# Inputs of a decoder layer laid out on the host: x by columns, parameters by columns, weights by loads

## The chip, the cores and the metric

One core of a Trainium2 chip runs the kernel. The metric is the device time in microseconds (us). Three runs of the kernel before are given by their median; one more run was profiled.

## The reference

One decoder layer on `x` (1 x 256 x 1024, float32). With one block of 256 keys, no past block can be chosen, so the block-sparse attention is causal attention over 16 heads of 64, with a relative-position bias on the logits. A gated feed-forward part with a causal width-3 depthwise convolution follows, and a last RMS norm.

```python
h = x
y = rms_norm(h, attn_norm)                    # x * rsqrt(mean(x^2) + eps) * g
q, k, v = split(y @ w_qkv)                    # 1024 -> 3 * 1024
s = q @ k.T * 64 ** -0.5 + bias(distance)     # causal
h = h + softmax(s) @ v @ w_o
y = rms_norm(h, ffn_norm)
u = conv3(y @ w_up) + conv_b                  # 1024 -> 2 * 2816, F = 2816
gate, val = split(u)
h = h + (silu(gate) * val) @ w_down           # 2816 -> 1024
out = rms_norm(h, final_norm)
```

## The kernel before, in words

Each product is made of three float32r products, high times high, low times high and high times low, so every weight is split into a high part (`whi`, on ACT, L175) and a low part (`wlo`, mostly on DVE, L194), and the activations too (`yt`, high on ACT at L298, low on DVE at L301). Weights come in loads of 1 MB into four `raw` buffers (`load`, L98), in a fixed order: four loads for v (each two blocks of 128 rows of the v part of `w_qkv`), then pairs for q and k (`qc`, `kc`, each 256 columns of all 1024 rows), then `w_o`, `w_up` and `w_down`. SP issues them; a load waits until its buffer has been split. The engines take their instructions in the order in which the program was recorded: nothing is reordered later.

The v product comes first. For each of the eight blocks of 128 features (k = 0 to 7), TensorE multiplies `yt` of that block with its weight rows into four accumulators `acc` (L349, L386): 12 products of 128x512 per block. `yt` needs x with features on partitions. x is loaded by rows (`xs`, L225), TensorE transposes it block by block against `ident` into a `bank` of PSUM (L289, L294), and ACT and DVE scale it by `g1` and split it from there. `g1` is `attn_norm` by columns: loaded as a row (L230), transposed (L259), scaled by ACT (L260). The other small vectors (`ffn_norm`, `conv_w`, `conv_b`) are loaded as `rows` (L246) and transposed in the middle of the v stage (`other_params`, L262).

The norm's factor is not needed for `yt`: it is put on q, k and v afterwards. `stat` gets the sums of squares of the two row halves of x from ACT (L428, L430), `rstds` (L276) turns them into `r1` with one DVE (L279) and one POOL instruction (L280), and just ahead of the products of the last block TensorE spreads `r1` over the partitions (`spread(r1, bank())`, L418, L286). After that, the first q and k products follow at once. Before the first product, TensorE runs some products of `ones` (`keep_warm`, L317).

At the end (L883 to L906) the last norm is put on four pieces of the output, and four DMAs store them: `by_final` (L853) multiplies a piece by `final_norm`, `weighted` (L841) does so for the rows of the second half, and `scale_of` (L847) gives the last factor `rf` through DVE (L849) and POOL (L850).

Of the kernel before, what the change touches and what calls it, by code (L numbers as in the profile page):

```python
# [14 lines left out]
P = 128  # L15
# [19 lines left out]
WARM = 6  # L35
MORE_WARM = 2
# [12 lines left out]
def tile_block(ctx: ExitStack, tc, x, attn_norm, w_qkv, w_o, rel_bias, ffn_norm, w_up, conv_w,  # L49
               conv_b, w_down, final_norm, out):  # L50
# [27 lines left out]
    wq, wo, wu, wd = w_qkv[0], w_o[0], w_up[0], w_down[0]  # L78
    ROWED = ("v", "o", "d", "s")
    first_tail = NG - TAIL  # L80
    blocks_of = wd[2 * first_tail * P:, :].rearrange("(i k p) (h c) -> k h p i c", k=2, p=P, h=2)
# [6 lines left out]
    def block(name):  # L88
        return blocks_of[int(name[0]) - 1, int(name[1]) - 1]

    def by_block(t):
        return t.rearrange("p (i c) -> p i c", i=TAIL)

    def add_block(t, name):
        more = block(name) if isinstance(name, str) else by_block(raws["s", name])
        nc.gpsimd.dma_start(by_block(t), more, accum_op=ALU.add)  # L96

    def load(key):  # L98
        kind, i = key
        if kind == "s":  # L100
            t = fp.tile([P, 2048], F32, name=f"sum{i}") if i in EARLY_SUMS else wraw.tile([P, 2048], F32, name="raw")
            nc.sync.dma_start(by_block(t), block(STAGES[i][0]))
            for name in STAGES[i][1:]:
                add_block(t, name)
            raws[key] = t
            return
        t = wraw.tile([P, 2048], F32, name="raw")
        if kind in ROWED:
            src = {"v": wq[:, 2 * D:], "o": wo, "d": wd}[kind][2 * i * P:2 * (i + 1) * P, :]
            dst, src = t.rearrange("p (k c) -> p k c", k=2), src.rearrange("(k p) c -> p k c", p=P)  # L110
        else:
            w, base = {"qc": (wq, 0), "kc": (wq, D), "gc": (wu, 0), "uc": (wu, F)}[kind]
            src = w[:, base + 256 * i:base + 256 * (i + 1)].rearrange("(k p) c -> p k c", p=P)
            dst = t.rearrange("p (k c) -> p k c", k=KD)
        if key == ("v", 0):
            load_x(0, 2 * P)
            for r in range(2):
                nc.sync.dma_start(dst[:, r, :], src[:, r, :])
            load_x(2 * P, 2 * P)
        elif key == ("v", 1):  # L120
            nc.sync.dma_start(dst[:, 0, :], src[:, 0, :])
            load_x(4 * P, 4 * P)
            nc.sync.dma_start(dst[:, 1, :], src[:, 1, :])
        else:
            nc.sync.dma_start(dst, src)
        raws[key] = t
# [50 lines left out]
    def split_lo():  # L177
        n, u = divmod(state["lo"], 2)
        if state["lo"] == state["hi"]:
            return  # L180
        state["lo"] += 1
        g = groups[n]
        src = parts(g)[u]
        lo[g, u] = wsp.tile([P, 1024], F32R, name="wlo", bufs=UNITS)
        if g in ADDED_LOW:
            nc.scalar.activation(lo[g, u], hi[g, u].bitcast(F32), AF.Copy, scale=-1.0)  # L186
            if g[0] == "d":
                k = 2 * g[1] + u
                nc.gpsimd.dma_start(lo[g, u], wd[k * P:(k + 1) * P, :], accum_op=ALU.add)
            else:  # L190
                nc.gpsimd.dma_start(lo[g, u].rearrange("p (i c) -> p i c", i=2),  # L191
                                    block(STAGES[g[1]][0])[:, 2 * u:2 * u + 2, :], accum_op=ALU.add)
# [32 lines left out]
    def load_x(b, n):  # L225
        c = slice(b, b + n)
        nc.sync.dma_start(xs[:, :, c], x[0, :, c].rearrange("(t p) c -> p t c", p=P))

    row1 = const.tile([KD, P], F32, name="row1")
    nc.scalar.dma_start(row1, attn_norm[0].rearrange("(k p) -> k p", p=P))  # L230
# [5 lines left out]
    rows = const.tile([P, 2, P], F32, name="rows")  # L236
# [3 lines left out]
    nc.vector.memset(rows[64:, :, :], 0.0)  # L240
    ROWS = {"w0": (0, 0), "w1": (0, 2 * NF), "g2": (0, 4 * NF), "w2": (1, 0), "b": (1, 2 * NF)}
    for name, src in (("g2", ffn_norm[0]), ("b", conv_b[0]), ("w0", conv_w[0, 0]), ("w1", conv_w[0, 1]),
                      ("w2", conv_w[0, 2])):
        i, r = ROWS[name]
        n = src.shape[0] // P
        nc.sync.dma_start(rows[r:r + n, i, :], src.rearrange("(k p) -> k p", p=P))  # L246

# [4 lines left out]
    params = const.tile([P, 2, P], F32, name="params")  # L252
    g2 = params[:, 0, 4 * NF:4 * NF + KD]

    g1 = const.tile([P, KD], F32, name="g1")

    def first_params():
        ps = bank()
        nc.tensor.transpose(ps[:, :KD], row1, ident[:KD, :KD])  # L259
        nc.scalar.activation(g1, ps[:, :KD], AF.Copy, scale=math.sqrt(D))  # L260

    def other_params():  # L262
        ps = spare()[:, :2 * P].rearrange("p (a b) -> p a b", a=2)
        for i in range(2):
            nc.tensor.transpose(ps[:, i, :], rows[:, i, :], ident)
        nc.scalar.activation(params, ps, AF.Copy)
        nc.scalar.activation(g2, g2, AF.Copy, scale=math.sqrt(D))
# [8 lines left out]
    def rstds():  # L276

        r = small.tile([P, NT], F32, name="rstd")
        nc.vector.scalar_tensor_tensor(r, stat[:, 0, :], D * EPS, stat[:, 1, :], op0=ALU.add, op1=ALU.add)  # L279
        nc.gpsimd.tensor_tensor(r, r, minus_half.to_broadcast([P, NT]), op=ALU.pow)  # L280
        return r
# [7 lines left out]
    def flipped_rows(k, ps=None):  # L289

        ps = (bank() if ps is None else ps).rearrange("p (a b) -> p a b", a=2)
        for a in range(2):
            for t in range(NT):
                nc.tensor.transpose(ps[:, a, t * P:(t + 1) * P], xt[t][:, (k + a) * P:(k + a + 1) * P], ident)  # L294
        return ps

    def columns_hi(ps, k, g, a):
        nc.scalar.activation(yt[:, 0, k + a, :], ps[:, a, :], AF.Copy, scale=g[:, k + a:k + a + 1])  # L298

    def columns_lo(ps, k, g, a):  # L300
        nc.vector.scalar_tensor_tensor(yt[:, 1, k + a, :], ps[:, a, :], g[:, k + a:k + a + 1],  # L301
                                       yt[:, 0, k + a, :].bitcast(F32), op0=ALU.mult, op1=ALU.subtract)

    def transposed(k, g, ps=None):

        ps = flipped_rows(k, ps)
        for part in (columns_hi, columns_lo):
            for a in range(2):
                part(ps, k, g, a)
# [12 lines left out]
    first_params()  # L322


    line = const.tile([H, LGT], F32, name="line")
    nc.gpsimd.memset(line[:, S:], NEG)
# [14 lines left out]
    att = ctx.enter_context(ExitStack())  # L341
    ap = att.enter_context(tc.tile_pool(name="ap", bufs=1))
# [52 lines left out]
    columns_lo(ps, 0, g1, 0)  # L395
    columns_hi(ps, 0, g1, 1)
    half_lo(0, 0)
    columns_lo(ps, 0, g1, 1)
    half_lo(0, 1)
    half_hi(1, 0, nc.scalar.copy)  # L400
    half_hi(1, 1, nc.vector.tensor_copy)
    for half in range(2):
        half_lo(1, half)
    for half in range(2):
        for n in range(2):
            first_products(half, hi, n)
# [3 lines left out]
    for i in range(4):  # L410
        if i < 3:
            transposed(2 * i + 2, g1)
        if i == 2:
            other_params()
# [12 lines left out]
        if i == 1:  # L427
            nc.scalar.activation(junk[0], xt[0], AF.Square, accum_out=stat[:, 0, 0:1])  # L428
        if i == 2:
            nc.scalar.activation(junk[1], xt[1], AF.Square, accum_out=stat[:, 0, 1:2])  # L430
            r1 = rstds()
# [51 lines left out]

    def weights():
        return ap.tile([P, 768], F32, name="weights", bufs=6)
# [167 lines left out]
    def squares(t, half):  # L653
        c = slice(half * 512, (half + 1) * 512)
        nc.scalar.activation(junk[t][:, c], xt[t][:, c], AF.Square, accum_out=stat[:, half, t:t + 1])
# [23 lines left out]
    def taps(col):  # L679
        return tuple(params[:, i, r + col:r + col + 1] for i, r in (ROWS[n] for n in ("w0", "w1", "w2", "b")))  # L680
# [197 lines left out]
    for o, c in lefts:  # L878
# [17 lines left out]
    by_final(nc.vector, c_last)  # L896
    nc.sync.dma_start(rows_of(0, left), xg[0][:, left])
    square(1, c_last, 1, last)
    r = scale_of(1, 1)
    weighted(1, c_last, last)  # L900
    c = slice(0, 576)
# [7 lines left out]
_INS = ["x", "attn_norm", "w_qkv", "w_o", "rel_bias", "ffn_norm", "w_up", "conv_w", "conv_b", "w_down",  # L909
        "final_norm"]  # L910
_OUTS = [((1, S, D), "float32")]

# [21 lines left out]
```

## Time and profile before

| what | value |
|---|---|
| median of three runs | 295.5 us (295.25 to 296.05) |
| profiled execution's own time | 295.74 us |
| its span in the profile | 293.9 us, granted TensorE clock 0.994 |
| TensorE (PE) | 285.8 us busy, 97% |
| VectorE (DVE) | 238.9 us busy, 81% |
| ScalarE (ACT) | 185.0 us busy, 63% |
| GpSimd (POOL) | 47.1 us busy, 16% |
| DMA | 71.51 MB in 48886 packets, mean 243 GB/s |
| first product of the v stage / first q product | 6.21 us / 30.28 us |
| last instructions issued | 290.28 us |

The profile's times count from the start of the span. The time of a run is 1.84 us more than the span in the profiled execution. Lines L... are those of the kernel before; the changed kernel has other numbers for the same lines, which are named where they are used.

### The profile page before, as it was taken

Reading aid. Unit: us, or ns where it says so; the run is one execution under the profiler, and the core shown is the slowest. Engines: PE = TensorE matmul, PEld = TensorE weight load, DVE = VectorE, ACT = ScalarE, POOL = GpSimd, SP = SyncE. Lnnn points to the kernel's source line nnn. Section 1 sums busy time; section 2 is a strip of 40 time slices with the busy share of each in tenths; the row PEclk is TensorE's granted clock in tenths of the full one; section 3 lists DMA queues with packets and bytes.
Section 4 is the critical chain, followed back from the end, with each engine's and each line's share of the span. In section 5 each row is a group of like instructions: output and inputs, shape, how many; then the busy total and the mean of one; then the engine's idle time right before and its main releaser. Section 6 shows DMA issues by size and latency. Waiting matters only on the chain.

```text
span 293.9 us, 5514 instructions
## 1 busy us (share of the span) xinstructions
PE 285.8 (97%) x2092; PEld 264.3 (90%) x2092; DVE 238.9 (81%) x449; ACT 185.0 (63%) x328; POOL 47.1 (16%) x72
## 2 busy tenths in 40 slices
PE   7999999999999999999999999999999999999991
PEld 6888999989978789998999899988999989998881
DVE  3866978679698586899899919999796997898884
ACT  4585746556564676477566807675449679955842
POOL 3905008329100002001000100000012002302001
PEclk9999999999999999999999999999999999999997
DMA  7999597898896862378995999849959986976303
GB/s 222 413 386 361 175 327 218 265 373 189 285 349 164 305 246 77 113 234 283 273 354 191 326 270 264 287 137 310 386 99 328 257 326 224 228 128 116 98 0 143
DMA packets 48886, 71.51 MB, mean 243 GB/s; under 512 B 1933, under 2 KB 37085, under 8 KB 48733
## 3 DMA queue, kind: packets, MB, share of 16 engines
q1 hardware_dynamic: 43564, 59.97, 59.6%
q0 software_dynamic: 3696, 9.99, 16.5%
q10 hardware_dynamic: 1600, 1.22, 1.6%
q8 instruction: 16, 0.26, 0.3%
q14 instruction: 10, 0.07, 0.1%
HBM read 66.29 MB, written 3.83 MB: 239 GB/s over the span
## 4 chain that ended last, share of the span: by engine, by line
PE 82%; issue 11%; ACT 2%; DMA 1%; POOL 1%; DVE 0%; POOLq 0%; SPq 0%; ACTq 0%
PE acc L74 37%; PE bank L74 37%; PE spare L74 7%; DMA raw<-in_w_qkv_dram 1%; ACT wlo L186 1%; PE acc L294 1%; PE bank L294 0%; POOL wlo L191 0%; POOL raw L833 0%; ACT whi L175 0%; ACT cv L729 0%; POOL raw L854 0%; DVE u L725 0%; ACT raw L891 0%; ACT raw L905 0%
## 5 line engine op out<-in xcount | busy, mean ns | idle before, releaser
L74 PE MATMUL bank<-yt,whi 128*128 128x256 f32 x704 | 120.3, 276 | 0.0
L74 PEld LDWEIGHTS bank<-yt,whi 128*128 128x128 f32 x704 | 105.9, 188 | 0.0
L175 ACT ACTIVATE whi<-raw 128x1024 fp32r<-128x1024 f32 x94 | 94.1, 1048 | 16.4 <-DMA raw<-in_w_qkv_dram 6.6
L194 DVE TENSOR_TENSOR wlo<-raw,whi 128x1024 fp32r<-128x1024 f32 x82 | 99.2, 1235 | 2.3 <-ACT whi L175 1.4
L74 PE MATMUL bank<-yt,wlo 128*128 128x256 f32 x352 | 97.2, 276 | 0.0
L74 PEld LDWEIGHTS bank<-yt,wlo 128*128 128x128 f32 x352 | 66.1, 188 | 0.0
L729 ACT ACTIVATE cv<-u,params 128x256 f32<-128x256 f32 x44 | 24.1, 594 | 50.7 <-DVE u L725 50.7
L74 PE MATMUL acc<-whi,at 128*128 128x512 f32 (+1 forms) x128 | 33.9, 383 | 0.0
L74 PEld LDWEIGHTS acc<-whi,at 128*128 128x128 f32 x128 | 23.5, 188 | 4.4
L74 PE MATMUL acc<-yt,whi 128*128 128x256 f32 x160 | 27.3, 276 | 0.0
L725 DVE TENSOR_TENSOR u<-bank,rb 128x512 f32<-128x512 f32 x22 | 15.1, 688 | 13.1 <-PE bank L74 13.1
L74 PEld LDWEIGHTS acc<-yt,whi 128*128 128x128 f32 x160 | 24.1, 188 | 0.0
L746 DVE SCALAR_TENSOR_TENSOR cv<-u,params,cv 128x254 f32<-128x254 f32 x44 | 21.3, 483 | 1.6
L74 PE MATMUL acc<-yt,wlo 128*128 128x256 f32 x80 | 22.1, 276 | 0.0
L744 DVE SCALAR_TENSOR_TENSOR cv<-u,params,cv 128x255 f32<-128x255 f32 x44 | 21.0, 478 | 0.7 <-ACT cv L729 0.7
L74 PE MATMUL acc<-whi,ot 128*128 128x512 f32 x64 | 20.2, 396 | 0.0
L74 PE MATMUL acc<-wlo,at 128*128 128x512 f32 (+1 forms) x69 | 20.0, 367 | 0.0
L74 PE MATMUL acc<-whi,yt 128*128 128x512 f32 x64 | 17.6, 399 | 1.1 <-DVE whi L380 1.1
L508 ACT ACTIVATE weights<-weights,nz 128x128 f32<-128x128 f32 (+1 forms) x32 | 14.1, 443 | 5.6 <-DVE nz L504 5.6
L74 PE MATMUL spare<-yt,whi 128*128 128x256 f32 (+1 forms) x96 | 16.8, 279 | 0.0
L96 POOL DMA_DIRECT2D sum<-in_w_down_dram x3 | 3.9, 1309 | 77.5 <-DVE wlo L194 55.8
L74 PEld LDWEIGHTS acc<-wlo,at 128*128 128x128 f32 x69 | 13.0, 188 | 2.6
(164 smaller groups left out, 401.7 us busy)
## 6 DMA issues: line engine op xcount, KB each, us to landing
raw<-in_w_up_dram SPq DMA_DIRECT2D x22, 1024.0 KB, 7.6
raw<-in_w_qkv_dram SPq DMA_DIRECT2D x10, 1024.0 KB, 8.2
raw<-in_w_down_dram SPq DMA_DIRECT2D x10, 1024.0 KB, 5.7
raw<-in_w_o_dram SPq DMA_DIRECT2D x4, 1024.0 KB, 5.7
sum<-in_w_down_dram SPq DMA_DIRECT2D x3, 1024.0 KB, 8.6
sum<-in_w_down_dram POOLq DMA_DIRECT2D x3, 1024.0 KB, 10.0
wlo<-in_w_down_dram POOLq DMA_DIRECT2D x6, 512.0 KB, 9.4
weights<-turned SPq DMA_DIRECT2D x7, 384.0 KB, 4.4
```

The costliest lines, as they stand in the source:

```text
L74: nc.tensor.matmul(o, lhsT, rhs, start=start, stop=stop, skip_group_check=True)
L96: nc.gpsimd.dma_start(by_block(t), more, accum_op=ALU.add)
L175: nc.scalar.activation(like(hi[g, u], src), src, AF.Copy)
L186: nc.scalar.activation(lo[g, u], hi[g, u].bitcast(F32), AF.Copy, scale=-1.0)
L194: state["by"].tensor_tensor(like(lo[g, u], src), src, like(hi[g, u].bitcast(F32), src), op=ALU.subtract)
L294: nc.tensor.transpose(ps[:, a, t * P:(t + 1) * P], xt[t][:, (k + a) * P:(k + a + 1) * P], ident)
L508: nc.scalar.activation(sc[p][:, a, c], sc[p][:, a, c], AF.Exp, bias=nm[:, j], accum_out=z[:, j])
L725: nc.vector.tensor_tensor(u, ps, rb2.unsqueeze(1).to_broadcast([P, 2, S]), op=ALU.mult)
L729: nc.scalar.activation(c[:, a, :], u[:, a, :], AF.Identity, scale=w2, bias=b)
L744: nc.vector.scalar_tensor_tensor(c[:, a, 1:], u[:, a, :S - 1], w1, c[:, a, 1:], op0=ALU.mult, op1=ALU.add)
L746: nc.vector.scalar_tensor_tensor(c[:, a, 2:], u[:, a, :S - 2], w0, c[:, a, 2:], op0=ALU.mult, op1=ALU.add)
```

## The change

Before the launch, `kernel()` now arranges the inputs with numpy: `x_cols` is x with features on partitions (128 x 8 x 256), beside x itself; `cols` holds all small vectors by columns (128 x 192); and the weights are arrays in which every load is one contiguous run of 8 KB per partition. In the program:

- The transposes of x for the v stage, those of the parameters, `row1`, `rows` and their loads are gone. `yt` is made from `x_cols` in SBUF (`column(k)`, held in three buffers that the attention uses later). The transposes of the second norm stay.
- ACT's queue issues the load of `cols` (into `params`) and then that of block 0 of `x_cols`. SP's queue issues the other blocks among the loads for v, and x by rows (`xs`, 1 MB), which only the sums of squares and the residual read, after the last load for v.
- Both sums of squares stand after the third pair of blocks (before: one after the second pair, one after the third). The factor 1/D goes into the squares in place of sqrt(D) in the gains.
- `WARM` is 8, in place of 6 and 2 more.
- At the end, the last `by_final` stands behind the last `weighted`, in place of ahead of the second `square`.
- Empty tiles (`lead`, `rest`, `pad`) shift addresses.

```diff
-        if key == ("v", 0):
-            load_x(0, 2 * P)
-            for r in range(2):
-                nc.sync.dma_start(dst[:, r, :], src[:, r, :])
-            load_x(2 * P, 2 * P)
...
+        pieces = {("v", 0): (512, 512, (1, 2), 1024, (2, 3)), ("v", 1): (1024, (3, 6), 1024, (6, KD))}.get(key, (2048,))
+        at_column = 0
+        for piece in pieces:
+            if isinstance(piece, tuple):
+                load_columns(nc.sync, *piece)
+            else:
+                c = slice(at_column, at_column + piece)
+                nc.sync.dma_start(t[:, c], src[:, c])
+                at_column = c.stop
+        if key == ("v", 3):
+            nc.sync.dma_start(xs, x[0].rearrange("(t p) c -> p t c", p=P))
...
-    row1 = const.tile([KD, P], F32, name="row1")
-    nc.scalar.dma_start(row1, attn_norm[0].rearrange("(k p) -> k p", p=P))
+    params = const.tile([P, 2 * KD + 8 * NF], F32, name="params")
+    nc.scalar.dma_start(params, cols)
+    load_columns(nc.scalar, 0, 1)
     load_next()
...
-    ps = flipped_rows(0)
-    keep_warm(MORE_WARM)
+    columns_hi(column(0), 0, g1)
     half_hi(0, 0, nc.vector.tensor_copy)
-    columns_hi(ps, 0, g1, 0)
     half_hi(0, 1, nc.scalar.copy)
...
     for i in range(4):
-        if i < 3:
-            transposed(2 * i + 2, g1)
-        if i == 2:
-            other_params()
+        for k in (2 * i + 2, 2 * i + 3):
+            if k < KD:
+                columns_hi(column(k), k, g1)
+                columns_lo(column(k), k, g1)
...
-        if i == 1:
-            nc.scalar.activation(junk[0], xt[0], AF.Square, accum_out=stat[:, 0, 0:1])
         if i == 2:
-            nc.scalar.activation(junk[1], xt[1], AF.Square, accum_out=stat[:, 0, 1:2])
+            for t in range(NT):
+                nc.scalar.activation(junk[t], xt[t], AF.Square, scale=D ** -0.5, accum_out=stat[:, 0, t:t + 1])
             r1 = rstds()
...
     weighted(1, c, y)
-    by_final(nc.vector, c_last)
-    nc.sync.dma_start(rows_of(0, left), xg[0][:, left])
     square(1, c_last, 1, last)
     r = scale_of(1, 1)
     weighted(1, c_last, last)
+    by_final(nc.vector, c_last)
+    nc.sync.dma_start(rows_of(0, left), xg[0][:, left])
```

How this moves instructions is seen at three places. In the rows below, `DMAHW0` to `DMAHW7` are the semaphores that the loads raise in turn, and a wait on one is a wait for a landing. First, the start of ACT's queue, before:

```order
L230 DMA row1_90<-in_attn_norm_dram 8x128
L260 ACT_TABLE_LOAD
L260 ACTIVATE g1_119<-bank_133 128x8 [waits PE_49]
L298 ACTIVATE yt_121<-bank_189,g1_119 128x256 [waits PE_49,Activation_49]
L380 CAST whi_185<-raw_92 128x512 [waits DMAHW2_49]
```

and now (`DMAHW2` is block 0 of `x_cols`, `DMAHW0` the parameters):

```order
L230 DMA params_97<-in_cols_dram 128x192
L227 DMA weights_94<-in_x_cols_dram 128x256
L276 ACT_TABLE_LOAD [waits DMAHW2_49]
L276 ACTIVATE yt_123<-weights_94,params_97 128x256 [waits DMAHW0_49]
L357 CAST whi_185<-raw_100 128x512 [waits DMAHW3_49]
```

ACT's table load stood in front of every wait; now it stands behind the landing of block 0 of `x_cols`. Second, ACT's queue in the second half of the v stage, before (`raw_103` is the last load for v, `raw_220` the first for q, `raw_251` the first for k):

```order
L175 ACTIVATE whi_292<-raw_103 128x1024 [waits DMAHW1_49]
L428 ACTIVATE junk0_124,stat_123<-xs_89 128x1024 [waits DMAHW6_49,DMAHW4_49]
L298 ACTIVATE yt_121<-bank_299,g1_119 128x256 [waits PE_49]
L298 ACTIVATE yt_121<-bank_299,g1_119 128x256
L266 ACTIVATE params_118<-spare_308 128x256 [waits PE_49]
L267 ACTIVATE params_118<-params_118 128x8 [waits Activation_49]
L175 ACTIVATE whi_337<-raw_103 128x1024
L175 ACTIVATE whi_341<-raw_220 128x1024 [waits DMAHW7_49]
L430 ACTIVATE junk1_125,stat_123<-xs_89 128x1024
L175 ACTIVATE whi_379<-raw_251 128x1024 [waits DMAHW0_49]
```

and now (`raw_113` the last for v, `raw_213` the first for q, `raw_239` the first for k):

```order
L166 ACTIVATE whi_275<-raw_113 128x1024 [waits DMAHW4_49]
L276 ACTIVATE yt_123<-weights_96,params_97 128x256 [waits DMAHW2_49]
L276 ACTIVATE yt_123<-weights_96,params_97 128x256
L166 ACTIVATE whi_309<-raw_113 128x1024
L166 ACTIVATE whi_313<-raw_213 128x1024 [waits DMAHW6_49]
L404 ACTIVATE junk0_126,stat_125<-xs_89 128x1024 [waits DMAHW5_49]
L404 ACTIVATE junk1_127,stat_125<-xs_89 128x1024
L166 ACTIVATE whi_352<-raw_239 128x1024 [waits DMAHW7_49]
```

Both squares now stand behind the split of the first q load, which SP issues behind `xs`. Third, the last instructions of DVE, before:

```order
L842 TENSOR_TENSOR raw_3349<-acc_1742,raw_3348 128x256
L854 TENSOR_TENSOR raw_3349<-raw_3349,raw_3348 128x256
L849 SCALAR_TENSOR_TENSOR rf_3523<-ends1_3352 128x1 [waits DVE_49,Activation_49]
L842 TENSOR_TENSOR raw_3349<-bank_3465,raw_3348 128x256
L902 TENSOR_SCALAR raw_3349<-raw_3349,rf_3523 128x576 [waits DVE_49,Pool_49]
```

and now:

```order
L814 TENSOR_TENSOR raw_3322<-acc_1715,raw_3321 128x256
L821 SCALAR_TENSOR_TENSOR rf_3494<-ends1_3325 128x1 [waits DVE_49,Activation_49]
L814 TENSOR_TENSOR raw_3322<-bank_3438,raw_3321 128x256
L826 TENSOR_TENSOR raw_3322<-raw_3322,raw_3321 128x256
L874 TENSOR_SCALAR raw_3322<-raw_3322,rf_3494 128x576 [waits DVE_49,Pool_49]
```

The factor `rf` now comes one instruction of 256 columns earlier, and the store of the left half of the first rows (L897) one or two later.

More of the change, by code (lines that the diff above doesn't have):

```diff
@@ L48, in tile_block @@
 @with_exitstack
-def tile_block(ctx: ExitStack, tc, x, attn_norm, w_qkv, w_o, rel_bias, ffn_norm, w_up, conv_w,
-               conv_b, w_down, final_norm, out):
+def tile_block(ctx: ExitStack, tc, x, x_cols, cols, w_v, w_qk, w_o, rel_bias, w_up, w_down, w_tail,
+               final_norm, out):
     nc = tc.nc
@@ L223, in tile_block, with weights, column, load_columns @@
     xt = [xs[:, t, :] for t in range(NT)]
-    def load_x(b, n):
-        c = slice(b, b + n)
-        nc.sync.dma_start(xs[:, :, c], x[0, :, c].rearrange("(t p) c -> p t c", p=P))
-    row1 = const.tile([KD, P], F32, name="row1")
-    nc.scalar.dma_start(row1, attn_norm[0].rearrange("(k p) -> k p", p=P))
+    att = ctx.enter_context(ExitStack())
+    ap = att.enter_context(tc.tile_pool(name="ap", bufs=1))
+    ap.tile([P, 48], F32, name="lead")
+    def weights():
+        return ap.tile([P, 768], F32, name="weights", bufs=6)
+    columns = [weights() for _ in range(3)]
+    def column(k):
+        return columns[k // 3][:, k % 3 * S:(k % 3 + 1) * S]
+    def load_columns(queue, k0, k1):
+        t, c = divmod(k0, 3)
+        dst = columns[t][:, c * S:(c + k1 - k0) * S]
+        queue.dma_start(dst.rearrange("p (k s) -> p k s", k=k1 - k0), x_cols[:, k0:k1, :])
+    params = const.tile([P, 2 * KD + 8 * NF], F32, name="params")
+    nc.scalar.dma_start(params, cols)
+    load_columns(nc.scalar, 0, 1)
     load_next()
@@ L250, in tile_block @@
     nc.gpsimd.memset(minus_half, -0.5)
[L252 to L267, printed above, removed]
+    g1, g2 = params[:, :KD], params[:, KD:2 * KD]
+    TAPS = [2 * KD + 2 * NF * n for n in range(4)]
     act.tile([P, 48], F32, name="skew")
@@ L308, in transposed @@
             for a in range(2):
[L309 removed]
+                part(ps[:, a, :], k + a, g)
     junk = [act.tile([P, D], BF16, name=f"junk{t}") for t in range(NT)]
@@ L321, in tile_block @@
     keep_warm(WARM)
-    first_params()
     line = const.tile([H, LGT], F32, name="line")
+    const.tile([P, 72], F32, name="rest")
     nc.gpsimd.memset(line[:, S:], NEG)
@@ L654, in squares @@
         c = slice(half * 512, (half + 1) * 512)
-        nc.scalar.activation(junk[t][:, c], xt[t][:, c], AF.Square, accum_out=stat[:, half, t:t + 1])
+        nc.scalar.activation(junk[t][:, c], xt[t][:, c], AF.Square, scale=D ** -0.5,
+                             accum_out=stat[:, half, t:t + 1])
     for t in range(NT):
@@ L922 @@
     arrays, args = {}, []
-    for name in _INS:
-        a = _np.ascontiguousarray(inputs[name])
+    for name, a in _laid({k: _np.asarray(v) for k, v in inputs.items()}).items():
+        a = _np.ascontiguousarray(a)
         arrays[f"in_{name}_dram"] = a
```

111 lines of the change are left out of this document (52 added, 59 removed).

## The prediction

> **What bounds the kernel now.** I read the page's busy times first, then what TensorE (PE) waited for, then the chain of work that ended last. PE is busy for 97% of the span, and its list of waits has two rows, both before the first product of the v stage:
>
> ```profile
> span 293.9 us, 5514 instructions
> PE 285.8 (97%) x2092; PEld 264.3 (90%) x2092; DVE 238.9 (81%) x449; ACT 185.0 (63%) x328; POOL 47.1 (16%) x72
> PE acc L74 <- DVE whi L380: 1.1, 1, 1.1
> PE spare L74 <- DVE ones L239: 1.0, 1, 1.0
> ```
>
> So from the first product to the last, PE has work ready all the time. The time is the start, plus PE's own stream, plus the tail. The other engines and the DMAs matter only where a change makes PE wait for them. The pieces of the chain in the v stage (start, length, what) show the stream, and which parts of it the change removes:
>
> ```profile
> 1.22 4.39 DMA raw<-in_w_qkv_dram
> ...
> 6.21 3.00 PE acc L74 x12
> 9.21 0.44 PE bank L294 x4
> ...
> 18.81 0.22 PE spare L265 x2
> 19.03 8.26 PE acc L74 x36
> 27.29 0.22 PE bank L286 x2
> 27.51 2.76 PE acc L74 x13
> 30.28 5.45 PE spare L74 x48
> ```
>
> **The change, part by part: PE's stream.** Of the four groups of transposes of x (L294), three lie in this stream, 0.44 each (the first at 9.21, and two more like it before 18.81), and the parameters' two (L265) take 0.22. That is 3 x 0.44 + 0.22 = 1.54 us less. The first group lay before 6.21. Without a new wait, PE would go from the first product to the spread of r1 (L286) in 27.29 - 6.21 - 1.54 = 19.54 us.
>
> **The start.** These rows show ACT's queue and PE before the first product, and then the time from issue to landing of two loads of x and two stores:
>
> ```profile
> 0.73 0.62 ACTq L230 DMA_DIRECT2D row<-in_attn_norm_dram  x1
> 1.38 1.28 ACT L260 ACT_TABLE_LOAD   x1 [1.38 <-PEq L921]
> 4.81 0.47 ACT L298 ACTIVATE yt<-bank,g 128x256 fp32r<-128x256 f32 x1 [0.47 <-PE bank L294]
> 6.21 2.08 PE L74 MATMUL acc<-whi,yt 128*128 128x512 f32 x8 [1.05 <-DVE whi L380]
> xs<-in_x_dram SPq DMA_DIRECT2D x2, 256.0 KB, 3.1
> out_dram<-raw SPq DMA_DIRECT2D x2, 256.0 KB, 2.0
> ```
>
> Before, the table load (1.28) was over long before data came. Now it waits for block 0 of `x_cols`. That load is ACT's second, issued at 0.73 + 0.62 = 1.35. Its landing is bounded by 2.0 (stores of 256 KB at the quiet end) and 4.39 (the first v load, 1.22 to 5.61). I take the 3.1 of the first loads of x, which met the same crowd: landing at 4.45. Then come the table load, 1.28, and the activation, 0.47: the first product at 6.2, as before, with ends at 5.1 and 7.5. The first product needs only half the first weights now, but the table load eats that. It will turn out that this term isn't on the path.
>
> **The factor r1.** The spread is in PE's order ahead of the last 12 products of the v stage. Today its inputs are early. Here are ACT's splits of the loads for v, which began when the load landed (the third at 14.51, the fourth at 17.30), and the chain to r1 behind the second square:
>
> ```profile
> 14.51 2.02 ACT L175 ACTIVATE whi<-raw 128x1024 fp32r<-128x1024 f32 x2 [0.70 <-DMA raw<-in_w_qkv_dram]
> 17.30 1.06 ACT L175 ACTIVATE whi<-raw 128x1024 fp32r<-128x1024 f32 x1 [0.78 <-DMA raw<-in_w_qkv_dram]
> 18.27 1.04 ACT L428 ACTIVATE junk<-xs 128x1024 bf16<-128x1024 f32 x1
> 22.45 1.04 ACT L430 ACTIVATE junk<-xs 128x1024 bf16<-128x1024 f32 x1
> 23.61 0.16 DVE L279 SCALAR_TENSOR_TENSOR rstd<-stat 128x2 f32<-128x2 f32 x1 [0.30 <-ACT junk L430]
> 23.86 1.64 POOL L280 TENSOR_TENSOR rstd<-rstd,minus_half 128x2 f32<-128x2 f32 x1 [8.31 <-DVE rstd L279]
> L286 PE MATMUL bank<-ident,rstd x2: 271/274/276, 27.1 to 27.2; 128*128 128x128 f32 x2
> ```
>
> From the start of the second square to the end of POOL's power are 25.50 - 22.45 = 3.05 us, and r1 then lies ready for 1.6 us until PE takes it at 27.1. In the new order both squares stand in ACT's queue behind the split of the first q load, and SP issues that load behind `xs`. So r1 is ready at the landing L of the first q load, plus 0.97 for the split (2.02 for two, less 1.06 for one, is the step), 1.04 for the first square, and 3.05: L + 5.06.
>
> Where does L lie? Up to the last v load the bytes in the queue stay: x was 1.05 MB and is 1.05 MB by columns, v is 4.19 MB, and 0.1 MB of small vectors by columns replaces as much by rows. So the last v load lands at 17.2 to 17.3 again. Then come `xs` and the first q load, 2.10 MB, where before only the q load came. The busy times by stretch (last three columns: granted clock, share of the DMA engines, GB/s) show the DMA engines full:
>
> ```profile
> 1.50:3.00 1.50, 1.50 (x9) 1.50 (x9) 0.00 (x0) 1.17 (x1) 0.89 (x3) 1.00 0.80 171
> 7.50:9.00 1.50, 1.50 (x8) 1.21 (x7) 1.50 (x4) 0.18 (x1) 1.50 (x3) 1.00 0.99 383
> 9.00:10.50 1.50, 1.50 (x10) 1.27 (x9) 0.62 (x2) 0.81 (x3) 1.50 (x10) 1.00 1.06 421
> 13.50:15.00 1.50, 1.50 (x8) 1.22 (x7) 1.50 (x3) 0.80 (x2) 1.23 (x4) 1.00 1.03 421
> 19.50:21.00 1.50, 1.50 (x9) 1.21 (x8) 0.84 (x3) 1.47 (x5) 0.00 (x0) 1.00 1.08 385
> 290.50:291.00 0.50, 0.00 (x0) 0.00 (x0) 0.00 (x0) 0.00 (x0) 0.00 (x0) 0.61 0.09 32
> ```
>
> From 9.0 to 15.0, when the v loads move in runs of 4 KB, it is 421 GB/s; from 19.5, when q and k loads move in runs of 1 KB, 385. The new loads have runs of 4 KB (`xs`) and 8 KB, so I take 421: 2.10 MB take 5.0 us, and L = 17.25 + 5.0 = 22.2. At 385 it would be 5.45 us, 0.45 later. The Trainium skill ("DMA: Bandwidth & Descriptors", Specifications) gives 512 B as the least transfer for full rate; by that rule 1 KB and 8 KB runs go equally fast, the 421 is no gain of length, and the forecast would be 0.45 us higher. The trace differs from it: 385 against 421 at full engines, so I keep the row.
>
> So r1 is ready at 22.2 + 5.06 = 27.3. PE has reached the spread at 6.2 + 19.54 = 25.8 and stands there for 1.5 us: the transposes that were saved turn into a wait. With a semaphore and the weight load (some 0.2 us, between nothing and the 0.3 which DVE shows as idle after ACT) the spread starts at 27.5 where it started at 27.1: 0.4 later, and with it all that follows. The start may lie anywhere in 5.1 to 7.5 without moving this: PE would come to the spread at 27.1 at the latest.
>
> **What is hidden.** `yt` from SBUF, ACT's and DVE's splits and the missing parameter copies lie beside PE's products; if a block were late, its price up to 1.5 us would go into the same wait. The 1.05 MB more from memory shows only through L. For all loads after the v stage, contiguous runs shorten transfers that PE never waits for: nothing, as long as the waits of PE stay empty. The five small loads that leave SP's queue are worth nothing, since the q load now waits for bytes ahead of it, not for SP. POOL's three bias loads stand behind r1 and start 2 us later; they are read only when the attention's scores are, two projections further on.
>
> **The tail.** The rows from the last factor to the end:
>
> ```profile
> 288.24 0.20 ACT L845 ACTIVATION_READ_ACCUMULATOR junk<-bank 128x1 f32 x1
> 288.44 0.41 DVE L854 TENSOR_TENSOR raw<-raw 128x256 f32<-128x256 f32 x1
> 288.77 0.14 DVE L849 SCALAR_TENSOR_TENSOR rf<-ends 128x1 f32<-128x1 f32 x1
> 288.92 0.36 SPq L897 DMA_DIRECT2D out_dram<-raw  x1
> 289.00 0.55 POOL L850 TENSOR_TENSOR rf<-rf,minus_half 128x1 f32<-128x1 f32 x1 [0.83 <-DVE rf L849]
> 289.58 0.52 DVE L902 TENSOR_SCALAR raw<-raw,rf 128x576 f32<-128x576 f32 x1 [0.33 <-POOL rf L850]
> 291.00:292.00 1.00, 0.00 (x0) 0.00 (x0) 0.00 (x0) 0.00 (x0) 0.00 (x0) 0.50 1.03 401
> ```
>
> The factor's DVE step (288.77) was held by `by_final` (288.44); now it can start with ACT's sum at 288.44 + 0.03. The last scaling starts 0.3 us earlier. But the store of 256 KB that went at 288.92 now goes at about 289.35, and its 0.65 us of moving at 401 GB/s then lie just ahead of the last 512 KB. Ends: a gain of 0.3 and nothing. I take 0.1, since the DMA engines are full in the last stretch.
>
> **Sum.** 0.4 later at the spread, 0.1 earlier at the end: +0.3 on the profiled 295.74. The median of the runs is 0.24 below that execution, and I put the difference on the median: 295.8 us.
>
> **The rivals.** First, faster: r1 comes before PE does. That needs L + 5.3 below 25.8, so L at 20.5, or 1.7 us earlier. For it: the first stretches moved only 171 to 383 GB/s; 7.44 MB at 421 from 1.5 on would be through at 19.2. Against it: the DMA engines were already 80 to 99% busy there, so a better rate needs cheaper packets, and the new first packets are as small (1 and 2 KB). Then the 1.54 us come through and the tail's 0.1: 295.5 - 1.6 = 293.9. Halfway cases lie between 293.9 and 295.2.
>
> Second, slower: the first q load lands later still, with `xs` in front of it at 385 GB/s and a start as slow as a table load behind the parameters makes it: 0.45 to 1.2 us more, 296.3 to 297.0. It decides for slower from L = 22.9.
>
> Third, slower through the clock: PE stands for some 1.5 us at the spread, and the granted clock may fall. In the row of 290.5 it is 0.61 and later 0.50, 2.6 us after the last product; after the gap of 1.05 us before 6.21 it was 1.00 again in every stretch. At half clock for as long as the fall took, 2.6 us, 1.3 us are added: 297.1. The Trainium skill ("TensorE: Matmul & The Clock Gate", HAM oscillation) warns of gaps above about 3.4 us in PE's work; by that rule this gap is too short, and the trace agrees at both ends, so it gets a small chance.
>
> **How the numbers follow.** About 0.3%, or 0.9 us, is what a measurement of this kernel can tell from no change. The forecast (0 to 0.8 later) has 0.48, r1 in time or nearly so 0.26, the late q load 0.17, the clock 0.09. For the range I go down to 293.9 and up to 297.0, which leaves part of the clock's case and the ends of the first rival outside. Faster takes most of the first rival, 0.24; slower the third and most of the second, 0.24; no change the rest, 0.52.
>
> **What the changed profile would show.** PE's waits should gain a row for the spread with POOL's power as releaser, about 1.5 us, and the spread should start near 27.5. ACT's table load should start after 3.3 us. ACT should wait for the first q load until about 22.2, with the squares right behind. The first q product should come at 30.7 in place of 30.28, and the spans from there to the last product should be equal. Wrong would be: no PE wait at the spread (then faster), a first product after 7.8, or PE waits after the v stage.

## The result, and the profile after

The changed kernel takes 298.21 us (median of 5, 297.94 to 299.66) against 295.46 for the kernel before (median of 5, 295.25 to 296.05): a ratio of 1.0101, 95% interval 1.0074 to 1.0127. It is slower by 2.7 us; the forecast was 295.8, with a range up to 297.0. The profiled execution took 298.64 us, its span 296.9. Three executions far from all others (416 and 303 us, with the granted clock at 0.66 and 0.94, and one of 750 us of the kernel before) are left out of the medians and ratios below.

PE's list of waits after. In place of the 1.1 us before the first product stands 3.1 us, a wait for the second fetch of the turned weights is new, and the row for the spread that was forecast is missing:

```profile
PE acc L73 <- ACT yt L276: 3.1, 1, 3.1
PE spare L73 <- DVE stat L324: 1.0, 1, 1.0
PE spare L73 <- DMA weights<-turned: 0.3, 1, 0.3
```

The chain of the first 37 us after (start, length, what). Block 0 of `x_cols` lands at 5.66, the table load begins only then, and the first product comes at 7.59 in place of 6.21:

```profile
1.17 4.49 DMA weights<-in_x_cols_dram
...
5.74 1.28 ACT L276
...
7.03 0.52 ACT yt L276
...
7.59 21.33 PE acc L73 x84
28.92 0.22 PE bank L264 x2
29.14 2.76 PE acc L73 x13
31.91 5.45 PE spare L73 x48
```

From the first product to the spread are 21.33 us, where 19.54 were forecast. The busy times by stretch tell why (PE's busy time and instructions come second, then weight loads, DVE, ACT, POOL; the last three columns are the granted clock, the DMA share and GB/s):

```profile
4.00:7.30 3.30, 0.51 (x4) 0.32 (x3) 0.43 (x1) 1.55 (x2) 1.14 (x8) 1.00 1.05 311
7.50:10.80 3.30, 3.21 (x8) 2.53 (x9) 3.23 (x7) 2.77 (x7) 3.30 (x9) 0.50 1.03 418
11.00:14.40 3.40, 3.40 (x16) 2.74 (x15) 3.13 (x5) 2.64 (x4) 3.40 (x8) 1.00 1.05 439
```

In the 3.3 us before the first product PE worked for 0.51, and the clock then stood at 0.50 for the next stretch: the first 8 products go at half clock, one every 0.43 us in place of 0.23. The granted clock was down for one step of 3.413 us, from 7.45 to 10.86. (A trace has no clock record ahead of the first change, at 4.03 here, and the view prints 1.00 there. The warm-up products show that the clock was at half until then: one every 0.21 us before, every 0.11 after.)

Without a fall and without a wait PE needs 19.5 us from the first product to the spread: so it is in two of the runs below, more warm-up alone and both. The transposes did leave the stream as reckoned, and 21.33 - 19.5 = 1.83 us were lost. Some 1.5 of them are the half clock (3.27 us from the first product on, at 0.43 a product in place of 0.23). The rest is slower products behind it: from 11.0 to 28.5 the trace has one every 0.2333 us, where the mean in the kernel before and in those two runs is 0.229. No row names a cause for that.

Where the 2.87 us lie by which the last products come later (241.47 before, 244.34 after, the chain's last 48 products at L73), from the chains of the two kernels:

| place | us |
|---|---|
| first product 7.59 in place of 6.21 | +1.38 |
| half clock up to 10.86, and slower products behind it (21.33 in place of 19.5) | +1.83 |
| transposes out of the stream (19.5 in place of 21.08) | -1.58 |
| the wait near 101 us, and gaps at it | +0.55 |
| two groups of products in the up stage (below) | +0.69 |

The up-stage groups, after; the same groups stood at 113.21 with 5.46 and at 118.89 with 13.64 before. The clock's record is 1.00 in both:

```profile
115.38 5.65 PE bank L73 x48
...
121.26 14.14 PE bank L73 x120
...
244.34 5.47 PE bank L73 x48
```

### The profile page after: what moved, and what is told of

Its sections match the earlier page's. It is cut to its first block, busy times and chain, and to the rows that moved or that the text cites. A ratio compares the mean times of both kernels' runs of the same rounds, so it can differ in the third digit from the quotient of the medians.

```text
span 296.9 us, 5467 instructions
## 1 busy us (share of the span) xinstructions
PE 286.3 (96%) x2073; PEld 264.4 (89%) x2073; DVE 237.9 (80%) x447; ACT 184.7 (62%) x326; POOL 47.7 (16%) x72
## 4 chain that ended last, share of the span: by engine, by line
PE 76%; issue 12%; DMA 4%; DVE 3%; ACT 3%; POOL 1%; ACTq 1%; POOLq 0%; DVEq 0%; SPq 0%
PE bank L73 36%; PE acc L73 32%; PE spare L73 7%; DMA weights<-in_x_cols_dram 2%; DMA turned<-weights 1%; DVE weights L469 1%; DMA weights<-turned 1%; ACT wlo L177 1%; DVE weights L498 1%; PE acc L272 1%; DVE weights L496 0%; ACT L276 0%; ACTq L484 0%; ACT whi L166 0%; ACT cv L701 0%
## 5 line engine op out<-in xcount | busy, mean ns | idle before, releaser
L73 PE MATMUL bank<-yt,whi 128*128 128x256 f32 x704 | 121.0, 277 | 0.0
L73 PEld LDWEIGHTS bank<-yt,whi 128*128 128x128 f32 x704 | 106.5, 188 | 0.0
L73 PE MATMUL bank<-yt,wlo 128*128 128x256 f32 x352 | 97.5, 277 | 0.0
L73 PEld LDWEIGHTS bank<-yt,wlo 128*128 128x128 f32 x352 | 66.1, 188 | 0.0
L73 PE MATMUL acc<-whi,at 128*128 128x512 f32 (+1 forms) x128 | 33.9, 383 | 0.0
L73 PEld LDWEIGHTS acc<-whi,at 128*128 128x128 f32 x128 | 23.5, 188 | 4.4
L73 PE MATMUL acc<-yt,whi 128*128 128x256 f32 x160 | 27.3, 276 | 0.0
L73 PEld LDWEIGHTS acc<-yt,whi 128*128 128x128 f32 x160 | 24.1, 188 | 0.0
L718 DVE SCALAR_TENSOR_TENSOR cv<-u,params,cv 128x254 f32<-128x254 f32 x44 | 21.3, 484 | 1.6
L73 PE MATMUL acc<-yt,wlo 128*128 128x256 f32 x80 | 22.1, 276 | 0.0
L73 PE MATMUL acc<-whi,yt 128*128 128x512 f32 x64 | 19.0, 427 | 3.1 <-ACT yt L276 3.1
L73 PE MATMUL acc<-whi,ot 128*128 128x512 f32 x64 | 20.1, 396 | 0.0
L73 PE MATMUL acc<-wlo,at 128*128 128x512 f32 (+1 forms) x69 | 20.0, 367 | 0.0
L73 PEld LDWEIGHTS acc<-whi,yt 128*128 128x128 f32 x64 | 13.0, 206 | 6.2 <-ACT yt L276 3.3
L73 PE MATMUL spare<-yt,whi 128*128 128x256 f32 (+1 forms) x96 | 16.8, 279 | 0.0
L73 PEld LDWEIGHTS acc<-wlo,at 128*128 128x128 f32 x69 | 13.0, 188 | 2.6
```

What stands on the lines that cost most here:

```text
L73: nc.tensor.matmul(o, lhsT, rhs, start=start, stop=stop, skip_group_check=True)
L718: nc.vector.scalar_tensor_tensor(c[:, a, 2:], u[:, a, :S - 2], w0, c[:, a, 2:], op0=ALU.mult, op1=ALU.add)
```

## The experiments

Theory A: the loss is the first product and the clock that falls because of the gap ahead of it; with these mended, r1 is what binds next. Rival B: it is made in later stages. Rival C: longer runs and other addresses slow the products. Each kernel was timed beside the kernel before; its medians there were 295.67 in the first group of four, 295.84 in the second and 295.83 in the third, and the ratios are to these runs. Beside the kernel after it was 295.46, so a difference of less than 0.4 us between kernels of different groups says nothing.

**The table load alone.** One activation that needs no data, ahead of the warm-up products, takes the table load out of the path.

```
+    nc.scalar.activation(junk[0][:, :1], ones[:, :1], AF.Copy)
     keep_warm(WARM)
```

> The changed kernel with one more ACT instruction, a copy of one column of ones, ahead of everything that waits for x: ACT's table load then comes at about 1.7 us and not behind the landing of block 0 of x_cols. Theory A (the start and the clock it costs): the first product comes 1.28 earlier, at about 6.3; the standstill of PE shrinks from 3.1 to 1.8 us, and the granted clock stays at 1.00; then the factor r1 (ready at 27.25 in the changed kernel) is the next to bind, and the spread starts at about 27.5 in place of 28.8: 296.8 us. Rival B (the loss is spread over later waits, such as the fetch of the turned weights near 100 us and slower products near 120 us): the start gives nothing lasting, and the time stays within 0.5 of 298.2. Rival C (addresses and longer runs in memory): no change either.

Measured: 297.64 us, ratio 1.0057 [1.0037, 1.0076]. The first product comes 0.97 earlier, after a gap of 1.80, and the spread needs the same 21.3 us as in the kernel after:

```profile
6.62 3.61 PE L73 MATMUL acc<-whi,yt 128*128 128x512 f32 x8 [1.80 <-ACT yt L276]
```

The first clock record begins only at 9.91 here. Until then the clock was at half, as the row shows: its 8 products took 3.61 us, where the kernel before needed 2.08 (row 6.21 of the prediction). The step of 3.41 us from 3.08 to 6.49 had been half idle (PE worked for 1.75), and the one up to 9.91 still ran at half clock. So the table's share came through, and the clock's did not.

**More warm-up alone.** PE has work until the data come.

```
-WARM = 8
+WARM = 22
```

> The changed kernel with 22 warming products in place of 8, and nothing else: PE works until about 7.4 us and hardly stands before the first product. Theory A: the first product stays at about 7.6, but the clock stays at 1.00, which saves 1.7 us of the v stage; the spread starts at about 27.4, now just bound by r1: 296.7 us. Rival B: the clock's half speed is only another form of waiting for r1 and for loads, so the v stage ends as before: 298.2. If the warming products are too many (the first product later than 7.8), they give back what they save.

Measured: 298.02, ratio 1.0073 [1.0047, 1.0098]. The clock stayed at 1.00 from 6.09 on, but the warm-up products went on until about 0.6 us after `yt` was ready (7.76), so the first product came at 8.37, and PE now waited 0.3 us at the spread (28.21) for r1. The forecast of 296.7 missed; this run shows that the fall can be avoided, not what it costs.

**Both.** The table load ahead and WARM = 16.

> Both: the early table load and 16 warming products. Theory A with r1 as the next bound: the first product at about 6.3 at full clock, PE at the spread at 25.8, but r1 only at 27.25: the spread at 27.5 and a wait of about 1.5 us there, so no better than either alone, 296.7 us. If r1 does not bind: 295.2 us. Rival B: 298 us.

Measured: 299.46, ratio 1.01 [1.0066, 1.0133]: no gain over the kernel after. The first product came at 6.78 at full clock, and then the wait of the prediction appeared, with a price that it had given only a small chance. PE's waits:

```profile
PE bank L264 <- POOL rstd L258: 2.1, 1, 2.1
```

The spread itself, and from the chain the 13 products behind it:

```profile
28.41 0.43 PE L264 MATMUL bank<-ident,rstd 128*128 128x128 f32 x2 [2.14 <-POOL rstd L258]
```

```profile
28.84 4.34 PE acc L73 x13
```

The stretches around the spread, with the columns as above:

```profile
26.10:29.40 3.30, 1.16 (x7) 0.86 (x7) 2.90 (x5) 2.23 (x4) 2.68 (x3) 1.00 0.74 313
29.50:32.80 3.30, 3.30 (x10) 2.53 (x9) 0.88 (x2) 0.69 (x1) 1.07 (x2) 0.50 0.84 220
33.00:36.30 3.30, 3.30 (x31) 3.30 (x30) 3.08 (x4) 3.30 (x4) 0.00 (x0) 1.00 0.19 27
```

From the first product to the start of the wait are 28.41 - 2.14 - 6.78 = 19.5 us. The gap of 2.1 us left PE busy for 1.27 of the 3.41 us of one step of the clock (from 26.05), and the next step, from 29.46 to 32.88, went at half: the 13 products took 4.34 us in place of 2.76, so one whole step costs 1.6 us. The gap at the start was gained, and paid again at the spread. Not in every execution: in three of the eight the mean clock was 0.994 to 0.997 and the time 297.3 to 298.1, in five 0.988 to 0.990 and 299.1 to 300.4.

**Both, and r1 earlier.** The squares of x go between the two units of the third round, so that they no longer stand behind the split of the q load:

```
-        if i:
+        if i == 2:
+            unit(1)
+            (both squares)
+            unit(1)
+        elif i:
             unit(2)
```

> As before, and the two squares moved ahead of the split of the first q load in ACT's queue (after the split of the last v load), so that r1 no longer waits for the first q load. r1 should be ready at about 24.1 (x by rows lands at 19.8, two squares 2.1, DVE and POOL 2.1), PE reaches the spread at 25.8 and does not wait: 1.6 us less than with the early table load and the warming products alone, 295.1 us against 298.2; against the kernel before 1.2 us less at the spread, so 294.2 if nothing is lost later. Which of the two it is says how much of the loss lies behind the v stage. If r1 was never the bound: the same time as the run before it.

Measured: 295.92, ratio 1.0003 [0.9983, 1.0023]. The move is worth 3.5 us against the run before it; the wait (2.1) and one step of half clock (1.6) add up to 3.7. No trace of this kernel at full clock is on record, so this is a sum that agrees, and not a wait seen to be gone; in the last kernel below, where the squares stand at the same place, PE does not wait at the spread. The expectation (294.2 to 295.1) was about 1 us lower.

**The squares alone.** The control for the last: the kernel after, with only that move.

> The kernel after with only the squares of x moved between the two units of the third round, so that r1 comes near 24.4 instead of 27.3. In the kernel after the transposes that spread r1 stand at 28.8 and wait for nothing, so by the theory of start and clock this alone gives nothing: 297.9 to 298.5. By the prediction's own step (r1 is what binds the spread) it would give some 0.4 us or more: 297.8 or less. If the ACT casts of the q weights behind it come too late, it is slower by up to 0.5.

Measured: 298.89, ratio 1.0111 [1.0094, 1.0128]: nothing gained. PE's waits:

```profile
PE acc L73 <- ACT yt L276: 3.2, 1, 3.2
PE spare L73 <- DVE stat L324: 1.0, 1, 1.0
PE spare L73 <- DMA weights<-turned: 0.2, 1, 0.2
```

So in the kernel after r1 binds nothing; it binds only once the start is mended (the table load and the warm-up). Both must go, and in either order the first alone shows no gain. The chain of this profile also tells the two parts of the 1.83 us apart: the clock was down for one step at nearly the same place (7.50 to 10.91), but the products behind it came at the usual 0.229 us, and the 84 products took 0.37 less than in the kernel after:

```profile
7.76 20.96 PE acc L73 x84
```

**The clock by itself, in the kernel before.**

```
-WARM = 6
-MORE_WARM = 2
+WARM = 1
+MORE_WARM = 0
```

> The kernel before with 1 warm-up product in place of 6 and 2: nothing else moves, and the first product still begins near 6.2. What the clock at the start is worth by itself. Theory A (the price of half clock): the clock rises after the first stretch of 3.4 us that is nearly filled with products, near 10.7 instead of 3.9, so products from 6.2 to 10.7 take twice as long, and 4.5 us of half clock cost 2.2 us: 297.2 to 297.8. If the products of the v stage wait for weights anyway, or the clock rises without full stretches: 295.5.

Measured: 298.06, ratio 1.0064 [1.004, 1.0088], 2.2 us over the kernel before. The first product came at 5.88, even a little earlier, and the first clock record begins only at 8.97. The chain shows the price: the first 12 products take 4.43 us, where the kernel before needed 3.00 (row 6.21 of the prediction), and the spread's 13 products start at 28.61 in place of 27.51.

```profile
5.88 4.43 PE acc L74 x12
...
10.76 2.77 PE acc L74 x12
...
28.61 2.76 PE acc L74 x13
```

The time lost at half clock is lost for good: the last 48 products begin at 242.57 in place of 241.47. The profiled execution (296.85) shows 1.1 us of it, the median 2.2: when the clock rises depends on where its steps of 3.4 us lie, and this kernel's runs spread from 296.57 to 299.91.

**Block 0 first on SP's queue.** To the kernel with both and r1 earlier, with WARM = 11:

```
-    load_columns(nc.scalar, 0, 1)
+    load_columns(nc.sync, 0, 1)
```

> The kernel after with the table load ahead, the squares of x earlier, 11 warm-up products, and now the first block of x by columns sent first on SP's queue instead of behind the parameters on ACT's. Theory A (first product and clock at the start, r1 next): the block lands near 3.5, the parameters (3.9 us from issue to landing) near 4.5, so the first product begins near 5.3 instead of 6.8 (the run with the table load and more warm-up products); the clock is up from about 4, r1 comes near 24.4 and the spread near 24.9, so no wait there. That is 1.5 us less than the 296.0 with the block on ACT's queue, 294.5; the second block of x (landing 6.4, needed at 7.4) may take 0.3 to 0.8 back: 294.5 to 295.3. Theory B (the loss lies in later stages): no less than 295.8, since what the start gains is lost before the second fetch of turned weights. Theory C (longer runs or addresses slow the products): 296.0 with the same start as A.

Measured: 297.51, ratio 1.005 [1.0034, 1.0066]: 1.6 us worse than with the block on ACT's queue (1.4, if each is taken against the kernel before beside it). Theory A's 294.5 is out; B's bound held, but not for B's reason. The next kernel has the same start, and its profile shows how:

```profile
5.38 0.72 PE L73 MATMUL acc<-whi,yt 128*128 128x512 f32 x2
7.06 1.65 PE L73 MATMUL acc<-whi,yt 128*128 128x512 f32 x6 [0.96 <-ACT whi L358]
8.55 1.08 PE L73 MATMUL acc<-wlo,yt 128*128 128x512 f32 x4
10.22 1.50 PE L73 MATMUL acc<-whi,yt 128*128 128x512 f32 x4 [0.59 <-ACT whi L358]
```

The first product did come at 5.4, but the weights behind the block do not come earlier: PE waits for the second half of the first ones and again for the next. ACT's split of that second half shows the landing, at 6.39 (at 6.33 it was there in the kernel with both); the next weights held ACT's split until 9.56, where it was 7.72 in that kernel:

```profile
6.39 0.62 ACT L358 CAST whi<-raw 128x512 fp32r<-128x512 f32 x1 [2.34 <-DMA raw<-in_w_v_dram]
```

An early first product alone is worth nothing if the second isn't ready.

**The fetch of turned weights.** In the kernel after, the fourth send of the second turn (on ACT's queue) lands 3.6 us after its issue, since the first fetch on SP's queue was issued at the same moment (94.24); the second fetch waits for it. In the kernel before, the first fetch was issued some 0.4 us behind the fourth send (93.0 and 92.6), and PE did not wait. The chain of the kernel after:

```profile
92.88 0.27 ACTq L484
...
94.19 3.58 DMA turned<-weights
...
98.23 0.03 SPq L506
...
98.32 3.16 DMA weights<-turned
...
101.61 0.87 PE spare L73 x8
```

Two kernels put that first fetch on ACT's queue, behind the sends: the one before this with it, and the kernel after with it alone.

```
     turn(last[1], rz[:, 4:8], nc.scalar)
-    fetch(last[0])
+    fetch(last[0], nc.scalar)
```

> The same as the kernel with the first block on SP's queue, and beside it the first fetch of the turned weights after the last scores issued on ACT's queue, behind the four sends of the second turn, instead of on SP's, where it overtook the fourth send (which then landed 3.6 us after its issue in the kernel after). If that overtaking is what makes the products wait near 101 us (0.55 us in the kernel after against before), this kernel is 0.4 to 0.6 us below the one with the first block on SP's queue: 294.0 to 294.8. If it is not, the two agree within 0.2 us. If the fetch on ACT's queue holds ACT's casts of the weights (three by 1.0 us) back from something due, it is slower by up to 0.6 us.

> The kernel after with only the first fetch of the last turned weights moved to ACT's queue, behind the sends of the second turn. If the fetch that overtakes the fourth send costs the 0.5 us near 101 us: 297.5 to 297.9, and no wait of PE there. If not: 298.2.

Measured: 297.19, ratio 1.004 [1.0025, 1.0055], 0.3 below the kernel without it; and 298.01, ratio 1.0079 [1.006, 1.0098], 0.2 below the kernel after (0.6, if each is taken against the kernel before beside it). In both profiles the wait near 101 us is gone. The second fetch followed the start of the four sends by 5.4 us in the kernel after (98.23 and 92.88 above), and by 3.5 with the fetch alone moved; these are ACT's and SP's queue rows there:

```profile
94.27 1.79 ACTq L484 DMA_DIRECT2D turned<-weights  x4
96.23 0.34 ACTq L506 DMA_DIRECT2D weights<-turned  x1
...
97.81 0.34 SPq L506 DMA_DIRECT2D weights<-turned  x1
```

The mechanism is shown by the traces; the gain in time agrees with it in sign, but the intervals overlap, so its size in the medians is not settled. With the fetch alone moved, the profile also has another start: the first clock record begins only at 13.00, and the first 12 products go at half clock.

**The weights by loads alone.** The kernel before with the weights laid out by loads; x, its transposes and the parameters stay.

```
-            src = wq[:, base + 256 * i:base + 256 * (i + 1)].rearrange(...)
+            dst, src = t, w[i, n]
```

> The kernel before with one part of the change alone: the weights laid out by loads (8 KB runs), while x, its transposes and the parameters stay as before. The prediction costs this part at nothing: 295.3 to 296.0. Theory C (the earlier fetch and the slower products between 115 and 135 us come with the longer runs): 296.2 to 297.0, with the products waiting near 101 us for the second fetch of turned weights as in the kernel after. If faster loads bring the first product earlier: 294.8 to 295.3.

Measured: 296.14, ratio 1.0012 [1.0, 1.0023]. PE's longest wait, and then rows of the chain:

```profile
PE acc L74 <- DVE whi L368: 1.5, 1, 1.5
```

```profile
6.64 2.99 PE acc L74 x12
...
30.67 5.45 PE spare L74 x48
...
113.60 5.46 PE bank L74 x48
...
119.28 13.64 PE bank L74 x120
...
241.86 5.47 PE bank L74 x48
```

The first product came 0.43 later than in the profile of the kernel before, and all else is 0.39 later to the end, with no wait near 101 us and the products as fast as before. So one half of theory C falls: longer runs cost nothing after the start. Other addresses are not tested by themselves; the last kernel below has the tiles of the kernel after and no slower products, which speaks against them. Whether the 0.4 at the start belongs to them is open, for the first product of kernels with the old loads also varies (6.21, and 5.88 in the one with less warm-up).

**The order at the end alone**, put into the kernel before.

```
-    by_final(nc.vector, c_last)
-    nc.sync.dma_start(rows_of(0, left), xg[0][:, left])
     square(1, c_last, 1, last)
     r = scale_of(1, 1)
     weighted(1, c_last, last)
+    by_final(nc.vector, c_last)
+    nc.sync.dma_start(rows_of(0, left), xg[0][:, left])
```

> The kernel before with the change's order at the end alone: the last by_final and its store behind the last squares, pow and weighted. The prediction's term is -0.1, between -0.3 and 0: 295.2 to 295.5. If the late store (L872 of the kernel after, 0.34 us of issuing on SP's queue right ahead of the next store) takes the gain back: 295.5 to 295.7.

Measured: 295.73, ratio 1.0002 [0.998, 1.0024]: nothing.

**The parts put together.** The table load ahead, WARM = 13, the squares earlier, the fetch on ACT's queue, and g1 and g2 apart from the taps, so that block 0 stands behind 64 B a row in place of 768:

```
-    nc.scalar.dma_start(params, cols)
+    nc.scalar.dma_start(params[:, :2 * KD], cols[:, :2 * KD])
     load_columns(nc.scalar, 0, 1)
+    nc.scalar.dma_start(params[:, 2 * KD:], cols[:, 2 * KD:])
```

> The kernel after with the table load ahead, 13 warm-up products, the squares of x earlier, the first fetch of the last turned weights on ACT's queue, and the parameters in two transfers: g1 and g2 (16 columns of 64 B a row) ahead of the first block of x by columns on ACT's queue, the taps behind it. SP's queue keeps the order of the kernel after. Theory A (start, clock, r1, fetch): the block lands about 1 us earlier than in the run with table load and more warm-up (5.9), so the first product begins near 5.8 instead of 6.8, without the waits for the second half of the first weights that came when the block went on SP's queue; with the fetch 0.4 us less: 296.0 - 1.0 - 0.4 = 294.6, below the kernel before. Theory B (two queues share one stream of engines, so whatever is put first delays the rest): the first product is early but waits follow in the v stage as with the block on SP's queue, and the time is 296.5 to 297.2.

Measured: 295.62, ratio 0.9993 [0.9976, 1.0009]. It beats the kernel after by 2.6 us, and is level with the kernel before. PE's first product, and then rows of the chain down to the last 48 products at L73:

```profile
6.31 2.17 PE L73 MATMUL acc<-whi,yt 128*128 128x512 f32 x8 [0.19 <-ACT yt L277]
```

```profile
4.66 6.12 DMA weights<-in_x_cols_dram
...
10.80 0.51 ACT yt L277
11.31 0.96 ACT whi L166
...
12.29 1.24 DVE wlo L181
...
13.57 13.11 PE acc L73 x56
26.68 0.22 PE bank L265 x2
...
240.86 5.47 PE bank L73 x48
```

The spread stands at 26.68 in place of 27.29. That is 20.4 us after the first product, where the stream alone takes 19.5: the x blocks 3 to 5, issued at 4.66, land at 10.78 and hold ACT's splits, DVE's behind them and through these PE, by some 0.9 us. That is where more than half of the transposes' 1.58 us goes now; the rest (0.61 at the last products) reaches the end of the profile, but the medians do not tell it from nothing.

## Why the prediction was wrong

**"This term isn't on the path"**, said of the start, is the step that failed. It was reckoned that PE would come to the spread at 27.1 at the latest, whatever the start, because PE would stand there anyway. That leaves out what a late start does to the clock: PE stood idle for 3.1 us, the clock fell, and the spread came at 28.92 in the chain, 1.63 later than before in place of 0.4. The clock was among the rivals, but at the wrong place and with the price of a gap at the spread (1.3 us, chance 0.09). In the runs one whole step cost 1.6. The v stage so makes up 1.23 of the 2.47 us by which the last products came later than forecast; the other 1.24 lie behind it (below).

**The start's own sum** had one term too small. It took the landing of block 0 from a row of another queue at another place (3.1 us) and got 4.45; it landed at 5.66, near the upper end that was written beside it. The block stands behind the parameters on ACT's queue and shares the engines with the first weights on SP's. The series landing, table load (1.28), activation (0.52) was right, and its sum with the upper end, 7.5, is near the 7.59 measured. At full clock this alone would have brought PE to the spread at 7.59 + 19.5 = 27.1, still ahead of r1.

**The mark for that chance** was drawn from a gap of 1.05 us that left the clock alone and one after the end, and "the trace agrees at both ends" misread the second: there the clock had fallen 2.6 us after the last product. The Trainium skill ("TensorE: Matmul & The Clock Gate", HAM oscillation) puts the limit for a gap at about 3.4 us; the traces differ: gaps of 3.1 us and of 2.1 us were followed by one step at half clock. What the Trainium skill says on the same page (The HAM clock gate) of a free-running window of 3413 ns fits them. The records change in steps of 3.413 us, and where the steps lie differs from trace to trace. Laid out by such steps (from each trace's first record, and back from it), PE's busy time in a step and the clock in the next one are:

| step begins at | PE busy, of 3.41 us | clock, then clock in the next step |
|---|---|---|
| after 4.03; squares alone 4.09; both 26.05 | 0.48; 0.44; 1.27 | 1.00, then 0.50 |
| before 3.89; weights by loads alone 4.00 | 2.36; 1.96 | 1.00, then 1.00 |
| less warm-up 2.15; table load alone 3.08; fetch alone 2.76 and 6.17 | 1.36; 1.75; 2.06 and 1.70 | half, then half |
| before 0.47; less warm-up 5.56; after 0.62 | 2.85; 3.08; 2.98 | half, then 1.00 |

So in these traces a step with 1.3 us of work or less lost the clock, one with 2.0 or more kept it, and the half clock at the start ended behind a step with 2.8 or more. The length of the gap would sort the falls as well (2.1 and 3.1 us against 1.1 and 1.5 that left the clock alone), and no run tells the two apart.

**The factor r1** was forecast to the tenth: L at 22.21 (22.2) and r1 ready at 27.27 (27.3), by these rows:

```profile
22.21 1.06 ACT L166 ACTIVATE whi<-raw 128x1024 fp32r<-128x1024 f32 x1 [2.20 <-DMA raw<-in_w_qk_dram]
25.63 1.64 POOL L258 TENSOR_TENSOR rstd<-rstd,minus_half 128x2 f32<-128x2 f32 x1 [8.99 <-DVE rstd L257]
```

But PE came to the spread at 28.8, so it did not bind; "no PE wait at the spread (then faster)" was wrong in its second half. With the start mended the wait came, 2.1 us in place of the 1.5 forecast, since L was 23.3 in that run.

**The stream** was right: 1.54 us forecast, 1.58 found (21.08 less 19.5). **The tail** was forecast at 0.1; the last power came 2.58 us later where the last products were 2.87 later, so 0.29 was gained on that chain (POOL's row at 291.58 in place of 289.00), and neither the span nor the edit by itself shows it.

**What was costed at nothing.** "Nothing, as long as the waits of PE stay empty" did not hold for the second fetch near 101 us: its price is 0.55 in the profile. The slower products (0.69, and some 0.3 in the v stage) have no row that names a cause. Those of the up stage were there in the profiles of the table load alone and of both, in a different stage (5.65 for the first 48 q products in place of 5.45) with more warm-up alone, with the squares alone and with the fetch alone, and not in the kernel before, with its loads alone changed, or with the parts put together. That stays open.

## What to carry to other kernels

Slack at a later wait does not make a late start free: ask first what the gap does to TensorE's clock, and reckon with a step of 3.4 us at half of it (1.6 us here). Work that is taken out of a bound engine's stream pays only when everything that stood beside it (here the first blocks, r1 and the x blocks behind them) is early by as much; where two waits lie in a row, mending the first alone can show nothing, so they are to be tried together and each by itself. And read the landing of a first load from a row of its own queue with its own neighbours, or forecast with the upper bound.

## What was not expected of the hardware

The clock fell after a gap of 2.1 us within running work. With block 0 first on SP's queue, so that x and the weights all came over one queue, the DMA engines were not fuller but emptier: from 4.0 to 6.4 us their share was 0.77 (213 GB/s), where it was 1.08 (379 GB/s) in the kernel with both, and the x blocks 3 to 5 held ACT until 12.11 in place of 10.22. And a fetch of 384 KB on one queue could hold the last 96 KB send on the other for 3.6 us, where the sends before took about 2.
